# A hand-written order of mixing steps: decays ahead of the second pair's projections, modulation rounds among the projections, softmax steps right behind them

## The chip, the cores and the metric

The kernel runs on one core of one Trainium2 chip. The metric is the device time of one execution in microseconds (us); a lower number is better. The engines named below are PE (TensorE, matrix products and transposes), DVE (VectorE), ACT (ScalarE), POOL (GpSimd) and SP (SyncE, which here only issues DMAs). Each of them works through its own queue in order, so an instruction that waits holds up all that stands behind it on the same engine. ACT, POOL and SP can also issue DMAs, and such an issue stands in the same queue.

## What is computed

Two layers of a diffusion backbone, on 512 latent tokens and, in the first layer, 256 context tokens with the same weights. Width 1024. One layer, cut to what matters here:

```python
def modulation(cvec, w_mod, b_mod):
    m = (jax.nn.silu(cvec) @ w_mod + b_mod)[..., None, :]
    return jnp.split(m, 6, axis=-1)

def trunk_layer(x, cx, c, c_ctx, ...):
    sh1, sc1, ga1, sh2, sc2, ga2 = modulation(c, w_mod, b_mod)
    sh1c, sc1c, ga1c, sh2c, sc2c, ga2c = modulation(c_ctx[None], w_mod, b_mod)
    u = (rmsnorm(x, g_mix) * (1 + sc1) + sh1) @ w_in
    uc = (rmsnorm(cx, g_mix) * (1 + sc1c) + sh1c) @ w_in
    p, gq, gk, gv, gg, rf, rb, aq, ak, av = split_in(u)
    ...
    # gated linear attention, both directions: decay = exp(cumsum(log_sigmoid(r @ w_gate + b_gate) / 16))
    o_gl, _, _ = gla_bidir(*gla_features(gq, gk, gv, rf, rb, w_gate, b_gate), s_f, s_b)
    # softmax attention of 8 heads over 256 context + 512 latent keys
    mix = jnp.concatenate([pool_mixer(p, w_pool, s_pool),
                           gla_output(o_gl, gg, g_gla, x.dtype),
                           latent_attention(ql, k_all, v_all)], axis=-1) @ w_out
    x = x + ga1 * mix
    x = x + ga2 * squared_relu_mlp(rmsnorm(x, g_mlp) * (1 + sc2) + sh2, w_up, w_down)
    # the first layer does the same for the context: cx = cx + ga1c * mix_c, ...
```

## The kernel before

All weights are float32 and are multiplied in three passes: each weight tile is loaded by a DMA of SP into a buffer of the tag `raw` (3 buffers), ACT rounds it to a high part `whi` (line 159), DVE makes the low part `wlo` as the difference (line 78), and PE does high times high, high times low and low times high. `whi` and `wlo` live in rings of the tags `hi` and `lo`.

A layer has a mixing part (input projections, gated linear attention, softmax attention, pooling, output projection) and an MLP part. In the profile below the mixing parts lie at about 60 to 457 us and 1030 to 1335 us, the MLPs behind them. In the mixing part four generators are interleaved by a string of letters in the table `STEPS`, one string for each layer; each letter lets its generator go on to its next `yield`, and the code that it passes is issued at that place:

- `a`: the projections, one token tile of 128 at a time: gates, keys and values (`k_proj`), queries (`q_proj`), and the pooled part (`p_proj`); outputs of the token-wise ones are named `tm` (line 335), those of the others `fm` (lines 316 and 318).
- `g`: the gated linear attention, in two pairs of heads. For each pair: `decay` (2 steps: the decays from `rT`, tiles `z` and `tree`), `levels` (8 steps, for the widths 0, 1, 2, 4, ... 64: matmuls `att`, line 763, then four in-place products on DVE that grow the query and key tiles `QQ` and `KK`, line 720, and a masked copy to `dg`, line 783, or copies to `AT`), `states` (2) and `outputs` (2). The order is decay, levels and states of pair 0, decay of pair 1, outputs of pair 0, then levels, states and outputs of pair 1. A level's matmuls read what the level before has grown.
- `m`: in the first layer only, the two remaining modulation rounds. A round is 8 steps; each step loads 1 MB of `w_mod` as two tiles `rawm` (SP, line 188, into the rings `hi` and `lo` that the weights use) and multiplies them into the PSUM tile `pm` (line 190), 4 instructions of PE for each tile. At the end of a round `mod_end` loads the bias into the tile `brow`, adds `pm` (line 199), transposes it (line 202), writes `modT` and stores the gates to DRAM (`gaD`, line 209). The first layer's MLP holds three more rounds, those of the second layer (`modulation_sums`), which end in the same function.
- `t`: the softmax attention. The first step makes the key stack: transposes `kT`, then `kh` on ACT and `kl` on DVE (line 78); the second makes the first query stack: transposes `qT`, then `qs` on ACT and DVE (line 78). Scores `sc` are at line 1020, the row maxima `nmx` at 1023, the exponentials `p` at 1024, their transposes `pT` at 1038, and the products with the values `av` at 1047.

At each `t` the loop first finishes all that is left of `a` (`run(at_)`) and of `m` (`run(mods)`). A scheduler then sets the final order on each engine, in which an instruction can move past others that it doesn't depend on; the rows of each engine shown under the change are that final order.

The query and key projections of pair 1 (`qk_proj(1, 0)` and `qk_proj(1, 1)`) stand ahead of the interleaved part, in the first layer ahead of `rT`, the transposed gate inputs that the decays read, in the second layer right behind it.

Of the kernel before, what the change touches and what calls it, by code (L numbers as in the profile page):

```python
# [10 lines left out]
F32 = mybir.dt.float32  # L11
# [13 lines left out]
LEVELS = (1, 2, 4, 8, 16, 32, 64)  # L25
C_GV, C_GG, C_R, C_AQ = 768, 1024, 1280, 1312
GT = 5
STEPS = ("aggaamgmagagaaagaaaamgaaaaamagaaaagaaaaaagmgaaaagamggmggmgtt"
         "mggtttmtttgttgtmgtggtttgtttgttmgtmtgttmgtt",
         "ggggagaggaaagaaggaaaaaagaaaagaaaggaagaaggatatgatttttgaatgttg"  # L30
         "tttgggtttgttggttttgtttgt")


@with_exitstack
def hybrid_kernel(ctx, tc, x, c, cx, c_ctx, w_mod, b_mod, g_mix, w_in, w_pool, s_pool, w_gate, b_gate,
                  g_gla, g_q, g_k, w_out, g_mlp, w_up, w_down, g_final, k_mask, k_rope, k_edge, k_invw, out):
    nc = tc.nc
# [3 lines left out]
    lay = ctx.enter_context(tc.tile_pool(name="lay", bufs=1))  # L41
    wp = ctx.enter_context(tc.tile_pool(name="wp", bufs=5))
# [9 lines left out]
    def nm(s):  # L52
        uid[0] += 1
        return f"{s}_{uid[0]}"
# [137 lines left out]
        mod_end(l, r, modT, pm)  # L192

    def mod_end(l, r, modT, pm):
        brow = lay.tile([128, 512], F32, tag="brow", name=nm("brow"))
        for j in range(4):
            c0 = r * 2048 + j * 512
            nc.scalar.dma_start(brow[32 * j:32 * j + 32], b_mod[l, c0:c0 + 512].partition_broadcast(32))
        V.tensor_tensor(brow, pm, brow, ALU.add)
        pt = psC("pt")  # L200
        for cc in range(4):
            T.transpose(pt[:, cc * 128:(cc + 1) * 128], brow[:, cc * 128:(cc + 1) * 128], ident)
        V.tensor_copy(modT[:, r], pt.rearrange("p (c j r) -> p j c r", c=4, j=4)[:, :, :, 0:2])
        if r >= 1:
            which = r - 1
            for s in range(2):
                for jj in range(2):
                    row = 32 * (jj + (2 if r == 2 else 0)) + s
                    nc.scalar.dma_start(gaD[l, which, s:s + 1, jj * 512:(jj + 1) * 512], brow[row:row + 1, :])

    def modulation_sums(l, r, modT, streams):

# [174 lines left out]
    def run(g):  # L387
        for _ in g:
            pass
# [24 lines left out]
    for l in range(2):  # L414
# [169 lines left out]
        def qk_proj(pr, qk, ps=None):  # L584
            isk = qk == 1
            if ps is None:
                ps = psA("fm")
                fm_matmul(ps, wcols(W, 256 + qk * 256 + pr * 128, 128, 1), hT, KT, True, both or isk)
            if isk:
                KK[pr] = wide("KK")  # L590
                A.activation(KK[pr][:, 0:NT], ps[:, 0:NT], AF.Copy)
                G.tensor_copy(KK[pr][:, NT:2 * NT], KK[pr][:, 0:NT])
            else:
                gq[pr] = slot("gq")
                A.activation(gq[pr][:, 0:N_], ps[:, 0:N_], AF.Copy, scale=0.125)
# [14 lines left out]
        for t in alltiles:  # L610
# [3 lines left out]
                ps = psB("tm")  # L614
                tm_matmul(ps[:, 0:288], t, wk, hT, KT)
            A.activation(GU[:, t], ps[:, 0:288], AF.Copy)
        if l == 0:
            qk_proj(1, 0)
            qk_proj(1, 1)

        rT = gp.tile([32, NT], F32, tag="gt", name=nm("rT"), bufs=GT)
        ps = psA("rT")
        for t in alltiles:
            T.transpose(ps[0:32, t * 128:(t + 1) * 128], GU[:, t, 256:288], ident)
        A.activation(rT, ps[0:32, 0:NT], AF.Copy)
        if l == 1:
            qk_proj(1, 0)
            qk_proj(1, 1)

        if l == 0:  # L630
            load_params(1)
# [4 lines left out]
        def gate_proj(pr):  # L636

            wk = wcols(W, C_GG + pr * 128, 128, 1)
            ps = psA("fm")
            fm_matmul(ps, wk, hT, KT, True, both)  # L640
            g_ = slot("gate")
            gx, tmp = g_[:, 0:N_], gslot("sg", "gt", bufs=GT)[:, 0:N_]
            A.activation(gx, ps[:, 0:N_], AF.Copy)
            gate[pr] = g_
            yield
            V.tensor_scalar(tmp, gx, -87.0, None, ALU.max)
            A.activation(tmp, tmp, AF.Exp, scale=-1.0)
            A.activation(tmp, tmp, AF.Ln, bias=one)
            A.activation(tmp, tmp, AF.Exp, scale=-1.0)
            V.scalar_tensor_tensor(gx, tmp, gglaT, gx, ALU.mult, ALU.mult)  # L650
# [224 lines left out]
        def k_proj():  # L875
            wk = wcols(W, C_AQ + 512, 256, 2)
            UK = slot("UK")
            UKt.append(UK)
            UV = slot("UV")
            UVt.append(UV)  # L880
            for t in alltiles:
                ps = psB("tm")
                tm_matmul(ps[:, 0:256], t, wk, hT, KT)
                A.activation(UK[:, t * 128:(t + 1) * 128], ps[:, 0:128], AF.Copy)
                A.activation(UV[:, t * 128:(t + 1) * 128], ps[:, 128:256], AF.Copy)  # L885
                yield
            sq = gslot("sq", "gt", bufs=GT)
            head_norm(UK.rearrange("p (m e) -> p m e", e=64), sq.rearrange("p (m e) -> p m e", e=64), 12)
            yield
            rope_mult(UK[:, 0:NL].rearrange("p (t h e) -> p t h e", h=2, e=64), rk,  # L890
                      sq[:, 0:NL].rearrange("p (t h e) -> p t h e", h=2, e=64), 4, 2)
            kc = UK[:, NL:NT].rearrange("p (m e) -> p m e", e=64)
            V.tensor_tensor(kc, kc, gr[:, 1].unsqueeze(1).to_broadcast([128, 4, 64]), ALU.mult)
            yield

        def q_proj(cb):
            wk = wcols(W, C_AQ + cb * 256, 256, 2)
            for t in live:
                g = t // 3
                if t % 3 == 0:  # L900
                    Uq[cb][g] = slot("Uq")
                uq = Uq[cb][g]
                ps = psB("tm")
                tm_matmul(ps[:, 0:256], t, wk, hT, KT)
                A.activation(uq[:, (t % 3) * 256:(t % 3) * 256 + 256], ps[:, 0:256], AF.Copy)
                yield
                if t % 3 == 2 or t == live[-1]:
                    nt = t % 3 + 1
                    sq = gslot("sq", "gt", bufs=GT)[:, 0:nt * 256]
                    uv_ = uq[:, 0:nt * 256]  # L910
                    head_norm(uv_.rearrange("p (m e) -> p m e", e=64), sq.rearrange("p (m e) -> p m e", e=64), nt * 4, 0.125)
                    yield
                    nr = nt if g == 0 else 1
                    u4 = uv_.rearrange("p (t h e) -> p t h e", h=4, e=64)
                    s4 = sq.rearrange("p (t h e) -> p t h e", h=4, e=64)
                    rope_mult(u4[:, 0:nr], rq[:, :, 3 * g:3 * g + nr], s4[:, 0:nr], nr, 4)
                    if nr < nt:
                        qc = uq[:, nr * 256:nt * 256].rearrange("p (m e) -> p m e", e=64)
                        V.tensor_tensor(qc, qc, gr[:, 0].unsqueeze(1).to_broadcast([128, (nt - nr) * 4, 64]), ALU.mult)
                    yield  # L920
# [8 lines left out]
            yield  # L929

        def a_thread():
            for th in (gate_proj(0), gate_proj(1), k_proj(), q_proj(0), q_proj(1), p_proj(0), p_proj(1)):
                yield from th

# [175 lines left out]
        for ch in STEPS[l]:  # L1110
            if ch == "t":
                run(at_)
                run(mods)
            next(ths[ch], None)
        run(at_)
        run(mods)
# [77 lines left out]
        mods = iter(())  # L1194
# [127 lines left out]
```

## Time and profile before

| | |
|---|---|
| median of 3 runs | 1698.22 us (1693.12, 1698.79, 1698.22) |
| the profiled execution: its own time | 1700.61 us |
| the profiled execution: its span on the core | 1698.8 us |
| instructions | 28409 |
| PE busy | 1618.9 us (95%) |
| DVE busy | 911.1 us (54%) |
| ACT busy | 639.1 us (38%) |
| POOL busy | 408.3 us (24%) |
| mean DMA rate | 96 GB/s |
| first layer, mixing to the output projection | about 60 to 385 us |
| second layer, mixing to the output projection | about 1030 to 1279 us |

The busy shares are means over the whole span, and the stages have different limits: in the MLPs PE hardly ever waits, in the mixing parts it does. PE's clock is granted by a throttle and is shown as a share of full speed. A row of the waits names an engine and a line, what ended its wait, and then the microseconds in total, the times and the longest one.

### The profile page before, as it was taken

The page shows a single profiled execution, that of the slowest core. Times are in us where ns is not written, and L with a number is a line of the kernel's source. Part 1 is how long each engine was busy: PE and PEld are TensorE (multiplying, and loading weights), DVE is VectorE, ACT ScalarE, POOL GpSimd, SP SyncE. Part 2 cuts the span into 40 slices and gives each one's busy share as a digit, 9 for nine tenths or more (in the row PEclk, how much of TensorE's full clock was granted, in tenths as well). Part 3 has the DMA queues.
Part 4 walks back from the last instruction along what each step waited for, and adds up shares of the span by engine and source line. Part 5 has one row for each costly group of instructions (what it writes and reads, how often), then busy time and mean ns, then how long its engine had stood idle before and what let it go on. Part 6 is the DMA issues. An engine that isn't in the chain of part 4 may idle for free.

```text
span 1698.8 us, 28409 instructions
## 1 busy us (share of the span) xinstructions
PE 1618.9 (95%) x11899; PEld 1334.4 (79%) x11899; DVE 911.1 (54%) x1302; ACT 639.1 (38%) x1092; POOL 408.3 (24%) x468
## 2 busy tenths in 40 slices
PE   7999968899999999999999999997899999999997
PEld 4989636669978888888888888885669888888885
DVE  4437367753583546546555564486753545545454
ACT  5444246662442312213122234454662522222222
POOL 1111031202201231220311362242111212222225
PEclk9999989999999999999999999997999999999999
DMA  9422530204331313325334232100024223333321
GB/s 320 125 87 65 204 107 3 101 13 127 98 122 53 124 54 121 130 63 186 119 98 161 87 104 81 55 2 1 2 98 126 86 76 99 99 100 99 100 99 50
DMA packets 140255, 163.36 MB, mean 96 GB/s; under 512 B 9412, under 2 KB 116304, under 8 KB 140128
## 3 DMA queue, kind: packets, MB, share of 16 engines
q1 hardware_dynamic: 133312, 147.10, 27.2%
q10 hardware_dynamic: 6816, 14.46, 2.4%
q8 instruction: 93, 1.52, 0.4%
q14 instruction: 34, 0.28, 0.1%
HBM read 157.31 MB, written 4.23 MB: 95 GB/s over the span
## 4 chain that ended last, share of the span: by engine, by line
PE 88%; DVE 4%; ACT 3%; DMA 2%; issue 2%; POOL 1%; SPq 0%; POOLq 0%; DVEq 0%; ACTq 0%
PE dn L335 25%; PE up L316 19%; PE tm L335 8%; PE op L335 7%; PE up L318 5%; PE fm L316 4%; PE av L1047 3%; PE pT L1038 3%; PE up L325 2%; PE fm L318 2%; PE sc L1020 1%; DMA rawm<-in_w_mod_dram 1%; PE att L763 1%; PE pm L190 1%; PE sc L1021 1%
## 5 line engine op out<-in xcount | busy, mean ns | idle before, releaser
L159 ACT ACTIVATE whi<-raw 128x1024 fp32r<-128x1024 f32 (+2 forms) x182 | 184.9, 1031 | 581.2 <-PE dn L335 294.5
L1177 POOL TENSOR_TENSOR X<-X,rtmp 128x512 f32<-128x512 f32 x158 | 215.8, 1368 | 653.5 <-DVE rtmp L1176 653.1
L78 DVE TENSOR_TENSOR wlo<-raw,whi 128x1024 fp32r<-128x1024 f32 (+2 forms) x182 | 224.9, 1245 | 240.2 <-ACT whi L159 237.2
L1176 DVE TENSOR_TENSOR rtmp<-dn,ga 128x512 f32<-128x512 f32 x160 | 109.5, 688 | 215.9 <-PE dn L335 213.0
L335 PE MATMUL dn<-whi,al 128*128 128x512 f32 x480 | 187.2, 390 | 0.0
L335 PE MATMUL dn<-whi,ah 128*128 128x512 f32 x480 | 187.1, 390 | 0.0
L335 PE MATMUL dn<-wlo,ah 128*128 128x512 f32 x480 | 186.3, 390 | 0.0
L316 PE MATMUL up<-h2h,whi 128*128 128x512 f32 x464 | 182.6, 394 | 1.5 <-ACT relu L1219 1.5
L316 PE MATMUL up<-h2h,wlo 128*128 128x512 f32 x464 | 183.2, 395 | 0.0
L316 PE MATMUL up<-h2l,whi 128*128 128x512 f32 x464 | 182.8, 394 | 0.0
L335 PEld LDWEIGHTS dn<-whi,ah 128*128 128x128 f32 x480 | 90.2, 188 | 20.3 <-DVE rtmp L1176 0.8
L316 PEld LDWEIGHTS up<-h2h,whi 128*128 128x128 f32 x464 | 87.1, 188 | 23.5 <-ACT relu L1219 2.5
L335 PEld LDWEIGHTS dn<-whi,al 128*128 128x128 f32 x480 | 90.1, 188 | 19.5
L335 PEld LDWEIGHTS dn<-wlo,ah 128*128 128x128 f32 x480 | 90.1, 188 | 18.9
L316 PEld LDWEIGHTS up<-h2l,whi 128*128 128x128 f32 x464 | 87.1, 188 | 21.8 <-issue 2.5
L335 PE MATMUL tm<-whi,hTh 128*128 128x256 f32 (+1 forms) x352 | 102.3, 291 | 1.1 <-ACT UV L885 1.1
L316 PEld LDWEIGHTS up<-h2h,wlo 128*128 128x128 f32 x464 | 87.2, 188 | 19.6
L335 PE MATMUL tm<-whi,hTl 128*128 128x256 f32 (+1 forms) x352 | 100.8, 287 | 0.0
L335 PE MATMUL dn<-whi,a 128*128 128x512 f32 x320 | 100.0, 395 | 0.4 <-DVE rtmp L1176 0.4
L335 PE MATMUL tm<-wlo,hTh 128*128 128x256 f32 (+1 forms) x352 | 100.0, 287 | 0.0
L335 PE MATMUL op<-whi,mixh 128*128 128x256 f32 x320 | 91.2, 285 | 0.9 <-ACT whi L159 0.9
L335 PE MATMUL op<-wlo,mixh 128*128 128x256 f32 x320 | 90.2, 283 | 0.3 <-DVE wlo L78 0.3
(289 smaller groups left out, 3480.5 us busy)
## 6 DMA issues: line engine op xcount, KB each, us to landing
rawm<-in_w_mod_dram SPq DMA_DIRECT2D x80, 512.0 KB
raw<-in_w_up_dram SPq DMA_DIRECT2D x64, 512.0 KB
raw<-in_w_down_dram SPq DMA_DIRECT2D x64, 512.0 KB
raw<-in_w_in_dram SPq DMA_DIRECT2D x26, 512.0 KB
rawm<-in_w_mod_dram SPq DMA_DIRECT2D x32, 256.0 KB
raw<-in_w_out_dram SPq DMA_DIRECT2D x16, 512.0 KB
raw<-in_w_in_dram SPq DMA_DIRECT2D x12, 256.0 KB
ga<-gaD ACTq DMA_DIRECT2D x6, 512.0 KB
```

The source lines that it names most:

```text
L78: V.tensor_tensor(lo, full, hi.bitcast(F32), ALU.subtract)
L159: A.activation(hi, raw, AF.Copy)
L190: T.matmul(pm[32 * j:32 * j + 32, :], sstat[:, k, :], raw[:, (j % 2) * 512:(j % 2) * 512 + 512], start=(k == 0), stop=(k == KT - 1), skip_ ...
L316: T.matmul(ps[:, 0:NL], a, b[:, 0:NL], start=st, stop=sp_)
L318: T.matmul(ps[:, NL:NT], a, b[:, NL:NT], start=st, stop=sp_)
L325: T.matmul(ps[:, cs], a, b[:, cs], start=(k == 0 and i == 0), stop=(k == nk - 1 and i == 2))
L335: T.matmul(ps, a[:, sl], bb, start=(k == 0 and i == 0), stop=(k == nk - 1 and i == 2))
L763: T.matmul(ps[g * bw:(g + 1) * bw, o0:o0 + bw], a_, b_, start=True, stop=True)
L1038: T.transpose(pt_[:, i * 128:(i + 1) * 128], p_[:, ki * 128:(ki + 1) * 128], ident)
L1047: T.matmul(av_[64 * hh:64 * hh + 64, 0:256], vst, pe[:, hh * 256:hh * 256 + 256], start=(ki == 0), stop=(ki == len(kts) - 1))
L1176: V.tensor_tensor(tmp, ps, ga[0 if t < 4 else 1][:, sl], ALU.mult)
L1177: (V if b == NB - 1 and not both and t == 3 else G).tensor_tensor(X[t][:, sl], X[t][:, sl], tmp, ALU.add)
```

## The change

1. `STEPS` has two new strings. In the first layer the old string has 33 `a`, 17 `g` and 8 of its 14 `m` ahead of the first `t`; the new one has 35 `a`, 20 `g` and all of its 17 `m`. In the second layer the old string has 25 `a` and 17 `g` ahead of the first `t`, the new one 31 `a` and 22 `g`.
2. The query and key projections of pair 1 move to the head of the projection generator, so that `rT` and the decays of pair 0 come ahead of them.
3. `run(mods)` at each `t` goes; what is left of the rounds would be done behind the loop, where nothing is left.
4. `brow` in `mod_end` takes a buffer of the weights' ring `raw` in place of its own; its four loads of the bias go from ACT's queue to SP's, and the four stores of the gates (in rounds 1 and 2) from ACT's queue to POOL's.

```diff
-STEPS = ("aggaamgmagagaaagaaaamgaaaaamagaaaagaaaaaagmgaaaagamggmggmgtt"
-         "mggtttmtttgttgtmgtggtttgtttgttmgtmtgttmgtt",
...
+STEPS = ("agamagamgaamgaagmaagmagamagamagamagagamagamagagamagamgaamgaagmaagmagamagam"
+         "ttgtgttgtgttgtttgttgttttgttttgtt",
...
     def mod_end(l, r, modT, pm):
-        brow = lay.tile([128, 512], F32, tag="brow", name=nm("brow"))
+        brow = wp.tile([128, 1024], F32, tag="raw", name=nm("brow"), bufs=3)[:, 0:512]
         for j in range(4):
             c0 = r * 2048 + j * 512
-            nc.scalar.dma_start(brow[32 * j:32 * j + 32], b_mod[l, c0:c0 + 512].partition_broadcast(32))
+            nc.sync.dma_start(brow[32 * j:32 * j + 32], b_mod[l, c0:c0 + 512].partition_broadcast(32))
...
-                    nc.scalar.dma_start(gaD[l, which, s:s + 1, jj * 512:(jj + 1) * 512], brow[row:row + 1, :])
+                    nc.gpsimd.dma_start(gaD[l, which, s:s + 1, jj * 512:(jj + 1) * 512], brow[row:row + 1, :])
...
-        if l == 0:
-            qk_proj(1, 0)
-            qk_proj(1, 1)

         rT = gp.tile([32, NT], F32, tag="gt", name=nm("rT"), bufs=GT)
...
-        if l == 1:
-            qk_proj(1, 0)
-            qk_proj(1, 1)
...
         def a_thread():
+            for qk in range(2):
+                qk_proj(1, qk)
+                yield
             for th in (gate_proj(0), gate_proj(1), k_proj(), q_proj(0), q_proj(1), p_proj(0), p_proj(1)):
                 yield from th
...
             if ch == "t":
                 run(at_)
-                run(mods)
             next(ths[ch], None)
```

On SP in the first layer, these rows stood around the last weights of the projections (`raw`; two `rawm` make one modulation step):

```order
L188 DMA rawm_1758<-in_w_mod_dram 128x1024
L152 DMA raw_2301<-in_w_in_dram 128x8x128
L188 DMA rawm_2182<-in_w_mod_dram 128x1024
L188 DMA rawm_2186<-in_w_mod_dram 128x1024
L188 DMA rawm_2384<-in_w_mod_dram 128x1024
L188 DMA rawm_2388<-in_w_mod_dram 128x1024
L188 DMA rawm_2437<-in_w_mod_dram 128x1024
L188 DMA rawm_2441<-in_w_mod_dram 128x1024
```

Six `rawm` of the 32 stood ahead of the last projection weights, `raw_2301`, and 26 behind them; 20 of those follow on the rows shown, in one run. In the changed kernel the rows around the last weights of the projections are:

```order
L152 DMA raw_2619<-in_w_in_dram 128x8x128
L152 DMA raw_2684<-in_w_in_dram 128x8x128
L188 DMA rawm_2181<-in_w_mod_dram 128x1024
L188 DMA rawm_2185<-in_w_mod_dram 128x1024
L188 DMA rawm_2260<-in_w_mod_dram 128x1024
L188 DMA rawm_2264<-in_w_mod_dram 128x1024
L188 DMA rawm_2307<-in_w_mod_dram 128x1024
L188 DMA rawm_2311<-in_w_mod_dram 128x1024
L188 DMA rawm_2449<-in_w_mod_dram 128x1024
L198 DMA brow_2806<-in_b_mod_dram 32x512 x4
L188 DMA rawm_2453<-in_w_mod_dram 128x1024
```

Now 18 `rawm` stand ahead of the last two projection weights, spread among the weights before them, and 14 behind; the bias loads come from this queue too.

On PE, just ahead of the first scores `sc` of the first layer, stood before (`rg` belongs to the outputs of pair 0, `att_2753` to the second level of pair 1):

```order
L202 MATMUL pt_2648<-ident,brow_2642 128x128 x3
L827 MATMUL rg_2527<-ident,rsg_2518 64x128 x8
L827 MATMUL rg_2538<-ident,rsg_2518 64x128 x4
L202 MATMUL pt_2648<-ident,brow_2642 128x128
L1073 MATMUL qT_2683<-ident,Uq_1537 128x128 x3
L1073 MATMUL qT_2683<-ident,Uq_1701 128x128
L1073 MATMUL qT_2684<-ident,Uq_1701 128x128 x2
L1073 MATMUL qT_2845<-ident,Uq_1537 128x128 x3
L1073 MATMUL qT_2845<-ident,Uq_1701 128x128
L763 MATMUL att_2753<-QQ_2550,KK_965 32x32 x48
L1020 MATMUL sc_2814<-kh_2669,qs_2691 128x512
```

And in the changed kernel:

```order
L190 MATMUL pm_2034<-rawm_2798,sstat 32x512 x2
L190 MATMUL pm_2034<-rawm_2802,sstat 32x512 x2
L976 MATMUL kT_2826<-ident,UK_1177 128x128 x6
L1070 MATMUL qT_2847<-ident,Uq_1626 128x128 x3
L1070 MATMUL qT_2847<-ident,Uq_1924 128x128
L1070 MATMUL qT_2848<-ident,Uq_1924 128x128 x2
L1070 MATMUL qT_3142<-ident,Uq_1626 128x128 x3
L1070 MATMUL qT_3142<-ident,Uq_1924 128x128
L757 MATMUL att_2865<-QQ_2446,kc_2866 32x32 x12
L202 MATMUL pt_2812<-ident,brow_2806 128x128 x4
L757 MATMUL att_2865<-QQ_2446,kc_2866 32x32 x36
L1017 MATMUL sc_2928<-kh_2833,qs_2855 128x512
```

Between the last projection and the scores stood 21 tiles of the modulation and the first two levels of pair 1 before (the rows shown are the end of it); now two tiles of the modulation do, and the levels are the third and fourth of pair 1 (from the third on they read `kc`, a copy of the keys). The outputs of pair 0 are done ahead of it.

On DVE, up to the first `qs` that those scores read, stood before:

```order
L720 TENSOR_TENSOR KK_965<-KK_965,z_2421 128x384
L720 TENSOR_TENSOR QQ_2550<-QQ_2550,z_2448 128x384
L783 COPY_PREDICATED dg_2552<-mask_735,att_2753 128x192 x2
L720 TENSOR_TENSOR KK_965<-KK_965,tree_2429 128x192x2
L720 TENSOR_TENSOR KK_965<-KK_965,tree_2456 128x192x2
L78 TENSOR_TENSOR kl_2670<-kT_2662,kh_2669 64x768
L720 TENSOR_TENSOR KK_965<-KK_965,tree_2429 128x96x4
L720 TENSOR_TENSOR KK_965<-KK_965,tree_2456 128x96x4
L78 TENSOR_TENSOR kl_2676<-kT_2662,kh_2675 64x768
L720 TENSOR_TENSOR KK_965<-KK_965,tree_2429 128x48x8
L720 TENSOR_TENSOR KK_965<-KK_965,tree_2456 128x48x8
L78 TENSOR_TENSOR qs_2691<-qT_2683,qs_2691 64x512
```

And in the changed kernel:

```order
L714 TENSOR_TENSOR QQ_2446<-QQ_2446,tree_2226 128x192x2
L714 TENSOR_TENSOR QQ_2446<-QQ_2446,tree_2279 128x192x2
L777 COPY_PREDICATED dg_2448<-mask_735,att_2741 128x192 x2
L199 TENSOR_TENSOR brow_2806<-pm_2034,brow_2806 128x512
L78 TENSOR_TENSOR kl_2834<-kT_2826,kh_2833 64x768
L203 COPY modT_124<-pt_2812 128x32
L383 SCALAR_TENSOR_TENSOR scT_125<-modT_124,vec 128x8 x2
L714 TENSOR_TENSOR QQ_2446<-QQ_2446,tree_2226 128x96x4
L714 TENSOR_TENSOR QQ_2446<-QQ_2446,tree_2279 128x96x4
L777 COPY_PREDICATED dg_2448<-mask_735,att_2865 128x192 x2
L78 TENSOR_TENSOR kl_2840<-kT_2826,kh_2839 64x768
L78 TENSOR_TENSOR qs_2855<-qT_2847,qs_2855 64x512
```

The products that grow `KK` here for the widths 1 to 8, and the two for the width 16 right behind these rows, stand further ahead now, beside the last projections; the products of `QQ` for the widths 2 and 4 stand here in their place, and the bias add `brow` has come in between.

More of the change, by code (lines that the diff above doesn't have):

```diff
@@ L27 @@
 GT = 5
-STEPS = ("aggaamgmagagaaagaaaamgaaaaamagaaaagaaaaaagmgaaaagamggmggmgtt"
-         "mggtttmtttgttgtmgtggtttgtttgttmgtmtgttmgtt",
-         "ggggagaggaaagaaggaaaaaagaaaagaaaggaagaaggatatgatttttgaatgttg"
-         "tttgggtttgttggttttgtttgt")
+STEPS = ("agamagamgaamgaagmaagmagamagamagamagagamagamagamagamgaamgaagmaagmagamagam"
+         "ttgtgttgtgttgtttgttgttttgttttgtt",
+         "agagaagagaagagaagagagaagagaagagaagagagaagagaagagaagag"
+         "ttgttgttgtttgtttgttttgttt")
 @with_exitstack
```

## The prediction

> **What bounds the kernel now.** I read the page first, then the windows by stage, then the waits of PE and of SP's queue, then the timelines around the two longest waits. On the page stand the span, PE's busy share in 40 slices and the chain that ended last:
>
> ```profile
> span 1698.8 us, 28409 instructions
> PE   7999968899999999999999999997899999999997
> PE 88%; DVE 4%; ACT 3%; DMA 2%; issue 2%; POOL 1%; SPq 0%; POOLq 0%; DVEq 0%; ACTq 0%
> ```
>
> PE makes 88% of the chain. A change that adds and removes no matmul can only take from the other 12%. Where they lie is seen in the windows (PE busy with its count, PEld, DVE, ACT, POOL, granted clock, DMA share, GB/s):
>
> ```profile
> 60.00:175.00 115.00, 115.00 (x1440) 103.33 (x1438) 54.31 (x91) 50.93 (x92) 17.86 (x34) 1.00 0.30 90
> 175.00:232.00 57.00, 53.00 (x493) 31.24 (x491) 21.20 (x48) 15.24 (x28) 8.29 (x18) 0.94 0.63 215
> 232.00:385.00 153.00, 128.56 (x1543) 90.68 (x1541) 102.17 (x176) 96.22 (x218) 30.02 (x48) 0.92 0.11 39
> 457.00:1000.00 543.00, 539.05 (x2771) 452.09 (x2770) 297.28 (x320) 138.08 (x164) 132.09 (x106) 1.00 0.34 112
> 1150.00:1280.00 130.00, 113.33 (x1243) 78.82 (x1242) 82.37 (x147) 79.50 (x164) 19.51 (x32) 0.92 0.12 42
> ```
>
> In the projections (60 to 175) PE is never idle. In 175 to 232 it is idle for 4.0 us, in the first layer's softmax stage for 24.4, in the second layer's for 16.7, each at a clock below 1. The first layer's MLP idles 4.0 us in 543. So 45 us at most are to be had in the stages that the change reorders, beside what the clock costs. What PE waits for, first layer (60 to 385), then second layer (1030 to 1290):
>
> ```profile
> PE sc L1020 <- DVE qs L78: 11.2, 1, 11.2
> PE sc L1020 <- ACT p L1024: 5.1, 4, 1.9
> PE pm L190 <- DMA rawm<-in_w_mod_dram: 3.9, 3, 3.5
> ...
> PE sc L1020 <- DVE qs L78: 4.5, 1, 4.5
> PE kT L979 <- ACT pm L927: 2.9, 1, 2.9
> PE att L763 <- ACT p L1024: 2.6, 3, 1.0
> ```
>
> Two single waits stand out in the first layer, 11.2 and 3.5 us; in the second the start of the softmax takes 4.5 and 2.9.
>
> **The 3.5 us wait, and what goes with it.** PE's timeline there, and from the chain a block of the same matmuls that waits for nothing:
>
> ```profile
> 174.11 1.06 PE L190 MATMUL pm<-rawm,sstat 128*32 128x512 f32 x8
> 181.19 1.92 PE L190 MATMUL pm<-rawm,sstat 128*32 128x512 f32 x4 [3.47 <-DMA rawm<-in_w_mod_dram]
> 184.26 0.63 PE L316 MATMUL fm<-hTl,whi 128*128 128x512 f32 x1
> 186.18 0.63 PE L316 MATMUL fm<-hTl,whi 128*128 128x512 f32 x1
> 187.47 0.40 PE L316 MATMUL fm<-hTl,whi 128*128 128x512 f32 x1
> 203.56 2.70 PE pm L190 x20
> ```
>
> The twenty matmuls of 174.11 to 183.11 (181.19 and its 1.92) take 9.0 us and cost 2.70 where nothing waits: 6.3 lost. Up to about 186.7 the projection's matmuls show 0.63 for what takes 0.40 later, and start every 0.43 instead of 0.23 us: half clock for 3.25 us, 1.6 lost. Together **7.9 us**. The cause is on SP's queue (60 to 240), whose waits are grouped by what freed the buffer:
>
> ```profile
> SPq L188 <- PE tm L335: 36.7, 4, 20.3
> SPq L188 <- PE pm L190: 23.2, 9, 16.0
> ```
>
> The modulation tiles use the weights' own buffers; one stood 20.3 us until a projection had read its weights. Once free, many loads come at once: DMA share 0.63 in 175 to 232 against 0.30 before. The new order puts 18 of the 32 tiles ahead of the last weights instead of 6. That moves 12 x 0.52 = 6.3 MB into a stretch that moved 90 GB/s x 115 us = 10.4 MB; 16.7 MB in 115 us are 145 GB/s, about half of the DMA engines' time by the share of that row (0.30 x 16.7 / 10.4 = 0.48). So the tiles can come in time, the burst behind the projections is gone, and I take all of the 7.9 off. Ends: nothing, if one tile is still late by as much, to 7.9.
>
> **The 11.2 us wait.** DVE in that stretch, then the prices of what stands there after the change, the last PE rows and the clock by windows of 10 us:
>
> ```profile
> 235.73 1.69 DVE L720 TENSOR_TENSOR QQ<-QQ,z 128x384 f32<-128x384 f32 x1 [0.68 <-PE att L763]
> 238.28 0.62 DVE L783 COPY_PREDICATED dg<-mask,att 128x192 f32<-128x192 int32 x2
> 238.97 1.94 DVE L720 TENSOR_TENSOR KK<-KK,tree 128x384 f32<-128x384 f32 x2
> 241.82 1.65 DVE L720 TENSOR_TENSOR KK<-KK,tree 128x384 f32<-128x384 f32 x2
> 243.51 0.96 DVE L78 TENSOR_TENSOR kl<-kT,kh 64x768 fp32r<-64x768 f32 x1
> 244.39 1.65 DVE L720 TENSOR_TENSOR KK<-KK,tree 128x384 f32<-128x384 f32 x2
> 246.07 1.02 DVE L78 TENSOR_TENSOR qs<-qT,qs 64x512 fp32r<-64x512 f32 x2
> L720 DVE TENSOR_TENSOR QQ<-QQ,tree 128x384 f32<-128x384 f32 x12 | 6.5, 571 | 5.7 <-PE att L763 5.7
> 233.45 1.25 PE L1073 MATMUL qT<-ident,Uq 128*128 128x128 f32 x10
> 234.63 1.06 PE L763 MATMUL att<-QQ,KK 64*32 64x32 f32 x96
> 1158.80 0.92 PE L979 MATMUL kT<-ident,UK 128*128 128x128 f32 x6 [2.89 <-ACT pm L927]
> 240.00:250.00 10.00, 3.10 (x10) 2.57 (x10) 9.77 (x15) 7.63 (x12) 2.99 (x6) 0.50 0.01 2
> 250.00:260.00 10.00, 5.74 (x117) 4.56 (x116) 9.65 (x17) 4.83 (x11) 0.72 (x4) 0.75 0.00 1
> ```
>
> Ahead of `qs` DVE grows `KK` for four widths in a row; that `KK` is not what the scores read, it only stands ahead of them in the queue. After the change these products lie beside the last projections. Behind the last projection PE then has a level (1.06), two modulation tiles (8 matmuls at 2.70 / 20, 1.1), `kT` (0.92), `qT` (1.25), four transposes of the bias tile (0.75, about 0.6 of `qT`'s row) and a level (1.06): 6.1 us. When that level is done, DVE still has two products of `QQ` (2 x 0.57), `dg` (0.62), `kl` (0.96) and `qs` (1.02): 3.7 us, which is PE's new idle time; everything before these on DVE fits into the 6.1. The saving is 11.2 - 3.7 = **7.5 us**. Ends: `kl` and `qs` alone (2.0, saving 9.2) and twice the estimate (7.4, saving 3.8), should DVE come into this stretch late.
>
> The clock is a separate matter. After 3.5 us of idle time it was half (181 to 186.7), and after the 11.2 us it was 0.50 and 0.75 in the two windows shown. With 3.7 us I expect it to halve again, so nothing is taken off for it.
>
> A rule of the Trainium skill bears on this point. TensorE: Matmul & The Clock Gate, in its part on the HAM clock gate, puts the fall to half clock after about 3.4 us of idle time and the return after about 3.4 us of sustained work. The trace agrees on the fall (3.47 us sufficed), while its return took 5.5 us. By that page an idle time of a little less than the 3.7 estimated here would keep full clock, and by the 5.5 us at half rate the sum would then be 2.7 us lower.
>
> **The rest of the first softmax stage.** In 250 to 260 PE is busy for 5.74 us and DVE for 9.65: DVE still sets the pace, with the backlog of `KK` and `QQ`. Without the eight products of `KK` (12 of them stood in this stage, below: 732 ns each, so 5.9 us) DVE reaches the row maxima earlier. Of the 4.3 us idle there I take **3 us** off; ends 0 and 5.9.
>
> ```profile
> L720 DVE TENSOR_TENSOR KK<-KK,tree 128x384 f32<-128x384 f32 x12 | 8.5, 732 | 0.1
> PE att L763 <- DVE QQ L720: 0.5, 1, 0.5
> 231.20 1.16 ACTq L209 DMA_DIRECT2D gaD<-brow  x4
> ```
>
> **What the projections pay.** Three more levels and the bias add now stand among them. DVE had 54.3 of 115 and 21.2 of 57 us to do there, so there is room; but each level reads what the one before has grown, and PE waits in order. A level is a chain of 1.06 (PE), 4 products at 0.57 and `dg` 0.62, some 4 us; twenty steps of this thread in about 150 us leave 7.5 us each, against 10 before (17 in 172). Where the spacing falls short, the nearest row is the wait of 0.5 us above. Four of them, **+2 us**; ends 0 and 8 (one stall like the 7.9).
>
> **Second layer.** No modulation runs there. The start now has `kT` and the scores behind levels four to six of pair 1; priced the same way, `kh` and `kl` twice, eight copies to `AT` on ACT and `qs` make about 7 us of idle time, as the 4.5 + 2.9 = 7.4 of before, so nothing is gained at the start. Behind it three level steps are left instead of eight. Of the 16.7 us idle in that stage 7.4 belong to the start; of the other 9.3, I take **4 us** off (5 of 8 levels gone, at 9.3 x 5 / 8 = 5.8, less a third for waits that stay between `sc`, `nmx` and `p`). Ends 0 and 9.
>
> **What I cost at nothing.** The moved `qk_proj` change only places. On ACT the stores of the gates took 1.16 us for four and delayed it ahead of `ogl`, but PE was still busy with the modulation; POOL, which takes them, is busy for 30 of 153 us. No row shows such an issue on POOL: between none and four times ACT's 1.16, beside that slack. `brow` in the weights' ring leaves two of three buffers to the weights for a few us, once in each of five rounds; in the MLP the DMA share is 0.34 and PE idles 4.0 of 543 us, so 0. The upper end is a late weight in each of the MLP's three rounds at 3.5 us, 10 us.
>
> **Sum.** -7.9 - 7.5 - 3 + 2 - 4 = -20.4 us. The profiled execution took 1700.6 us, the median of three 1698.2; the same change from the median gives **1678 us**, 1.2% less. What a measurement can tell from no change is about 0.5%, 8.5 us.
>
> **Rivals.**
>
> 1. *Only the late tiles are cured.* The scores come earlier, but DVE is then just as late: it has nearly the same work (102 of 153 us) in a shorter time, and the 11.2 us come back in pieces. For it: DVE at 9.7 of 10 us around the start. Against: the products that stand ahead of `qs` are really fewer. 1698.2 - 7.9 = 1690 us.
> 2. *Slower: the modulation tiles hold up SP's queue ahead of weights.* A tile may only be loaded when a projection has given up its buffer, and the weights of a later projection now stand behind it in SP's queue in 12 more cases. The row with 20.3 us shows that such a wait is long. If weights then come late, PE stands still in the middle of the projections, where it never waited before, and each such stall has the measured price of 7.9 us, half clock and all. It turns the sum from the third one on and is past 0.5% with four: 1678 + 31.6 = 1710 us. Against it: the order asks for every weight before the tiles that follow it, and 115 us of projections without a wait show that weights come early.
> 3. *Nothing comes of it.* The time won at the two waits is given back at the end of the stage, because with fewer levels to fill in, PE waits for ACT and DVE (`p` and `nmx`) between scores: 5.1 us of such waits stand there now, and they would have to grow fourfold. 1697 us.
>
> **How the numbers follow.** Forecast 0.60, rival 1 0.17, rival 2 0.10, rival 3 0.13. Faster by over 0.5% is below 1689.7: the forecast and half of rival 1, 0.69. Slower: rival 2, 0.10. Within 0.5%: the rest, 0.21. The range takes the larger ends of the terms on the good side (7.9 + 9.2 + 5.9 + 9 without a cost would be 1666; a little below it if the clock holds, 1663) and on the bad side rivals 1 and 3 with a margin, 1702; it leaves rival 2 out.
>
> **What would show it.** The wait of `pm` for `rawm` is gone, and no wait over 1 us stands in the projections (steps one and four). The first `sc` of the first layer waits for 2 to 5 us, with `QQ` and not `KK` ahead of `qs` on DVE. The stage from that `sc` to the output projection is shorter by some 3 us, and that of the second layer by some 4. The MLPs keep their length to 1 us. A `tm` or `fm` that waits for `wlo` or a load, or MLPs that are longer, would make the prediction wrong.

## The result, and the profile after

| | median | runs | lowest to highest |
|---|---|---|---|
| before | 1698.31 us | 4 | 1693.12 to 1698.79 |
| changed | 1707.12 us | 4 | 1706.6 to 1707.72 |

The ratio is 1.0059, 95% interval 1.0039 to 1.0079: the changed kernel is 0.6% slower, where 1.2% faster was forecast. The profiled execution took 1707.13 us, 6.5 more than that of before. The span on the page and PE's busy time, which has hardly changed (1618.9 before):

```profile
span 1704.9 us, 28427 instructions
PE 1620.6 (95%) x11899; PEld 1336.7 (78%) x11899; DVE 911.3 (53%) x1302; ACT 639.6 (38%) x1092; POOL 415.7 (24%) x484
```

The windows of the changed kernel, with the columns of those shown of before:

```profile
60.00:175.00 115.00, 113.15 (x1464) 93.75 (x1463) 56.57 (x102) 49.61 (x92) 18.92 (x32) 1.00 0.48 161
175.00:232.00 57.00, 56.48 (x782) 43.16 (x780) 30.96 (x60) 23.95 (x38) 17.25 (x29) 1.00 0.24 76
232.00:385.00 153.00, 135.23 (x1310) 96.67 (x1311) 95.03 (x159) 93.33 (x213) 27.49 (x48) 0.94 0.16 54
457.00:1000.00 543.00, 539.05 (x2731) 450.29 (x2730) 293.46 (x315) 139.56 (x168) 139.96 (x118) 1.00 0.34 110
1030.00:1150.00 120.00, 107.36 (x1297) 94.38 (x1296) 65.89 (x124) 54.06 (x105) 28.72 (x56) 0.93 0.13 36
```

The first layer looks as it was meant to. In 175 to 232 PE is idle for 0.5 us instead of 4.0, at full clock, and the DMA share of the projections rose from 0.30 to the forecast 0.48. The last row stands for the second layer's projections: PE idled 2.3 us of these 120 before (117.73 busy, row below), now 12.6, and the clock fell to 0.93. PE's waits, first layer (60 to 385), then second layer (1020 to 1180):

```profile
PE sc L1017 <- ACT p L1021: 5.5, 4, 1.8
PE sc L1017 <- DVE qs L78: 4.1, 1, 4.1
PE pT L1035 <- ACT p L1021: 2.6, 1, 2.6
PE pm L190 <- DMA rawm<-in_w_mod_dram: 1.3, 1, 1.3
...
PE sc L1017 <- DVE qs L78: 6.1, 1, 6.1
PE kbt L688 <- DVE KK L714: 4.5, 1, 4.5
PE tm L335 <- ACT UV L879: 2.6, 1, 2.6
PE att L757 <- ACT kc L738: 2.1, 1, 2.1
PE att L757 <- DVE QQ L714: 1.9, 3, 0.9
PE att L757 <- DVE KK L714: 1.7, 2, 1.3
```

The two single waits of the first layer shrank (`qs` 11.2 to 4.1, `rawm` 3.9 to 1.3); the waits of the scores for `p` did not (5.1 before, 5.5 now). In the second, a series of waits for the level chain has come, ahead of a softmax start that waits about as long as before.

Where the span went is seen best from four marks in each trace: the first `op` of the first layer, the first `tm` of the second layer, its first `op`, and the end. All later comparisons use the same marks:

| us | to the first layer's `op` | to the second layer's `tm` | to its `op` | to the end |
|---|---|---|---|---|
| before | 384.3 | 648.0 | 246.8 | 419.7 |
| changed | 372.9 | 647.3 | 265.7 | 419.0 |
| difference | -11.4 | -0.7 | +18.9 | -0.7 |

The first layer's mixing won 11.4 us, the MLPs stayed, and the second layer's mixing lost 18.9. Between the first `rT` and the first `sc` of the second layer the trace before has 111.9 us, the changed one 136.0; from there to `op` the changed one has 108.8 against 114.1. The stretch from `rT` to `sc` in the windows, changed and before:

```profile
1041.10:1177.10 136.00, 113.70 (x1530) 97.32 (x1528) 78.50 (x159) 62.02 (x125) 31.52 (x56) 0.92 0.11 32
```

```profile
1053.10:1165.00 111.90, 102.43 (x1210) 87.68 (x1207) 66.91 (x131) 56.72 (x112) 33.36 (x53) 0.98 0.14 39
```

PE idles 22.3 us there instead of 9.5, 12.8 more. It works at half clock for 15.4 us instead of 1.0; half of the difference, an estimate of 7.2 us, is lost by that. The 320 more matmuls are five more levels of pair 1, 3.8 us at 0.76 each. Together that is 23.8 of the 24.1 us.

The worst place is at 1104 to 1118 us. PE's timeline there in the changed kernel, then DVE's and ACT's (start, duration, engine, line, what, and in brackets the idle time ahead of it with what ended it):

```profile
1104.69 0.76 PE L757 MATMUL att<-QQ,kc 64*32 64x32 f32 x64
...
1108.69 0.33 PE L757 MATMUL att<-QQ,KK 64*64 64x64 f32 x4 [1.35 <-DVE KK L714]
1109.40 0.68 PE L757 MATMUL att<-QQ,KK 64*64 64x64 f32 x28 [0.38 <-DVE KK L714]
1114.63 3.12 PE L688 MATMUL kbt<-ident,KK 128*128 128x128 f32 x12 [4.55 <-DVE KK L714]
```

```profile
1108.80 0.55 DVE L714 TENSOR_TENSOR KK<-KK,tree 128x384 f32<-128x384 f32 x1
...
1111.51 0.17 DVE L260 SCALAR_TENSOR_TENSOR rsa<-rsa,ssa 128x12 f32<-128x12 f32 x1 [1.70 <-ACT rsa L258]
...
1112.33 0.96 DVE L867 TENSOR_TENSOR Uq<-Uq,rsa 128x768 f32<-128x768 f32 x1
...
1113.54 0.95 DVE L714 TENSOR_TENSOR KK<-KK,tree 128x384 f32<-128x384 f32 x1
```

```profile
1109.29 0.30 ACT L257 ACTIVATE rsa<-ssa,epsc 128x12 f32<-128x12 f32 x1
1109.50 1.73 ACT L770 ACTIVATE AT<-att 32x128 f32<-32x128 f32 x8
1111.26 0.21 ACT L258 ACTIVATE rsa<-rsa 128x12 f32<-128x12 f32 x1
```

The last three levels of pair 0 and the transposes `kbt` follow each other on PE with no projection tile in between. The first of the three doesn't wait; the other two and `kbt` each wait for a product on DVE, 7.2 us together (0.93, 1.73 and 4.55). The last product stands on DVE behind the query norm (`rsa`, `Uq`), which waits 1.70 us for ACT, where eight copies to `AT` stand between the norm's two steps. In the trace before, 3.1 to 4.0 us of projections stood between any two of these levels and ahead of `kbt`, and none of them waited:

```profile
1107.33 0.76 PE L763 MATMUL att<-QQ,kc 64*32 64x32 f32 x64
...
1111.44 0.76 PE L763 MATMUL att<-QQ,KK 64*32 64x32 f32 x64
...
1116.02 0.69 PE L763 MATMUL att<-QQ,KK 64*64 64x64 f32 x32
...
1119.63 1.47 PE L694 MATMUL kbt<-ident,KK 128*128 128x128 f32 x12
```

PE's clock pays as well. The same 10 us in the windows of the changed kernel, then of before, here with the row of the whole stretch:

```profile
1110.00:1120.00 10.00, 5.36 (x41) 4.49 (x38) 7.19 (x15) 3.53 (x12) 3.08 (x4) 0.50 0.01 2
```

```profile
1110.00:1120.00 10.00, 10.00 (x168) 9.62 (x167) 8.63 (x17) 8.11 (x26) 2.54 (x4) 1.00 0.01 3
...
1030.00:1150.00 120.00, 117.73 (x1269) 104.24 (x1270) 67.43 (x132) 58.97 (x118) 36.21 (x64) 1.00 0.14 40
```

### The profile page after: what moved, and what is told of

It is laid out like the page before. It is cut to its first block, busy times and chain, and to the rows that moved or that the text cites. A ratio compares the mean times of both kernels' runs of the same rounds, so it can differ in the third digit from the quotient of the medians.

```text
span 1704.9 us, 28427 instructions
## 1 busy us (share of the span) xinstructions
PE 1620.6 (95%) x11899; PEld 1336.7 (78%) x11899; DVE 911.3 (53%) x1302; ACT 639.6 (38%) x1092; POOL 415.7 (24%) x484
```

## The experiments

Each run is compared with runs of the kernel before on the same chip; the medians of before beside them were 1697.98, 1700.01 and 1697.08 us, so ratios are the surer numbers. Medians and ratios, and the marks of each profiled execution:

| run | median us | ratio, 95% interval | first layer's `op` | second layer's `tm` to `op` |
|---|---|---|---|---|
| before | | 1 | 384.3 | 246.8 |
| changed | 1707.12 | 1.0059 (1.0039 to 1.0079) | 372.9 | 265.7 |
| e1_l2_old | 1687.65 | 0.9927 (0.9913 to 0.9941) | 374.0 | 244.7 |
| e2_l2_new_alone | 1713.69 | 1.0085 (1.0070 to 1.0100) | 381.4 | 263.8 |
| e5_l2_spaced | 1699.50 | 0.9997 (0.9987 to 1.0008) | 372.9 | 257.5 |
| e7_l1_mod_alone | 1699.20 | 1.0005 (0.9992 to 1.0017) | 382.6 | 244.8 |
| e6_l1_levels_burst | 1694.47 | 0.9971 (0.9960 to 0.9983) | 378.2 | 246.3 |
| e4_brow_back | 1704.85 | 1.0033 (1.0021 to 1.0046) | 372.4 | 262.8 |
| e10_l2_early_levels | 1687.31 | 0.9931 (0.9919 to 0.9943) | 373.8 | 244.1 |
| e11_stacks_early | 1687.03 | 0.9938 (0.9926 to 0.9951) | 374.4 | 244.1 |
| e12_brow_back | 1686.41 | 0.9938 (0.9925 to 0.9950) | 370.2 | 246.1 |
| e13_l2_gates_first | 1701.61 | 1.0023 (1.0014 to 1.0033) | 372.2 | 261.2 |

A mark comes from one execution. Where PE's rows are the same it still moves by 2 to 3 us (first layer: 384.3 before, 381.4 in e2; second layer: 244.1 in e10, 246.1 in e12), so smaller differences between marks say little.

**The second layer as before, and its change alone.** First the changed kernel with the second layer's part undone:

```diff
-         "agagaagagaagagaagagagaagagaagagaagagagaagagaagagaagag"
-         "ttgttgttgtttgtttgttttgttt")
+         "ggggagaggaaagaaggaaaaaagaaaagaaaggaagaaggatatgatttttgaatgttg"
+         "tttgggtttgttggttttgtttgt")
...
         A.activation(rT, ps[0:32, 0:NT], AF.Copy)
+        if l == 1:
+            qk_proj(1, 0)
+            qk_proj(1, 1)
...
-            for qk in range(2):
+            for qk in range(2 if l == 0 else 0):
```

> The changed kernel with the second layer as before (its old string in STEPS, its two qk_proj behind rT again); the first layer's new order, the bias tile in the weights' ring and the moved DMAs stay. Theory (the second layer's order costs what is lost): the second layer gives back the 18.7 us by which it became longer, so 1707.1 - 18.7 = about 1688 us, 10 us under before. Rival 1 (the ring, the queues or the earlier end of the first layer spoil the second layer whatever its order): still 1700 us or more. Rival 2 (half of it is the order): about 1697 us.

And the reverse, the kernel before with this part alone:

> The kernel before with nothing but the second layer's part of the change (new second string, its two qk_proj at the head of the projections). Theory: the first layer is as before and the second one longer by 18.7 us: about 1717 us, more than the whole change costs. Rival 1 (the loss needs the bias tile in the ring or the first layer's new order): 1698 us.

1687.65 and 1713.69 us: both on the side of the theory. The second layer's order alone costs 0.85% (14 us; 17.0 by the marks), less than the 18.7 expected, and the rest of the change alone gains 0.73% (12 us). The loss needs neither the ring nor the first layer.

**Which part of the second layer's order.** In the first try its letters are shifted, with a projection tile that has matmuls behind each late level of pair 0:

```diff
-         "agagaagagaagagaagagagaagagaagagaagagagaagagaagagaagag"
-         "ttgttgttgtttgtttgttttgttt")
+         "agagaagagaagagaagaaagagagaaagaaagagagaaagaagaggaga"
+         "ttgttgttgttgttgttgttgttgttttt")
```

> The changed kernel with the letters of the second layer's new string shifted, so that each level of pair 0 from the fourth on has a projection tile with matmuls behind it; ahead of the first t stand 31 a and 19 g instead of 31 a and 22 g. Theory (PE stands still because levels follow each other with no projection in between): the 7.0 us of waits at the last levels of pair 0 and the half clock behind them (3 to 5 us) go, about 1695 to 1698 us. Rival (too much work for DVE and ACT among these projections, however it is spread): within 3 us of 1707.

1699.5, 0.6% less than the changed kernel by the two ratios and 1.5 us above the theory's range: the rival falls, but 10.7 us of the second layer's loss stay (257.5 against 246.8). The levels start as late here as in the change, 36.7 us behind `rT` (23.7 before), so the late start alone doesn't make the loss: from `rT` to `sc` 11.7 us came back (136.0 to 124.3), 2.3 of them for three levels of pair 1 that now stand behind that `sc`. The cover is still short: in PE's order 14 matmuls stand between the last two levels, and none between the last one and `kbt`. Waits that are left, second layer:

```profile
PE sc L1015 <- DVE qs L76: 7.1, 1, 7.1
PE tm L333 <- ACT UV L877: 2.6, 1, 2.6
PE kbt L686 <- DVE KK L712: 2.0, 1, 2.0
```

Two suspects are left: the early part of the string, and the levels of pair 1 ahead of the softmax. The second layer of e1 was given three such levels among its last projections, the rest as before:

```diff
-...gaagga" "tatgatttttgaatgttgtttgggtttgttggttttgtttgt"
+...gaagga" "aagagaga" "ttttttttttgtttgggtttgttggttttgtttgt"
```

> The kernel with the first layer's new order and the second layer's old one (1687.7), but with three levels of pair 1 of the second layer put among its last projections instead of behind the first softmax steps; the levels of pair 0 and the gates keep their old places. Theory (the loss that is left in the spaced order, 12 us, comes from the early part: gates in one piece ahead of the levels, and ACT late for the keys): 1685 to 1690. Rival (levels of pair 1 ahead of the softmax cost what they were to save, since they put DVE work ahead of qs): 1693 or more.

1687.31 us, a ratio of 0.9931 beside e1's 0.9927: the levels of pair 1 cost nothing there and bring nothing. The first `sc` behind them waits longer (6.8 us instead of 4.6), behind it 4.3 us come back (112.0 to 107.7 from there to `op`). Nearly as many steps stand ahead of the softmax here as in the change (20 `g` against 22). So the loss is in where the steps of pair 0 stand. The sharpest form of that is one edit in e10: the two gate projections ahead of the first seven `g` and not among them, as the change has them:

```diff
-"ggggagaggaaagaaggaaaaaag...
+"aagggggggaaagaaggaaaaaag...
```

> The fastest version so far (1687.3) with one edit in the second layer's string: its two letters for the gate projections (11.5 us of matmuls) stand ahead of the first seven letters g instead of among them, as they do in the change. Number and kind of steps ahead of the softmax are the same. Theory (a projection covers a level's wait only if its letter stands behind that level): the levels start later, the last three stand in a row again, and 4 to 9 us are lost, 1691 to 1696. Rival (only the number of levels ahead of the softmax counts): 1687 within 2.

1701.61 us, 14 us more than e10 (0.9% by the ratios), past the upper end of the theory's range: the direction and the place are the theory's, the size is more than twice its middle. From `rT` to `sc` PE idles 19.6 us instead of 11.9, at a mean clock of 0.89 instead of 0.98. PE's waits ahead of the softmax in e10 (1020 to 1150), then in e13 (1020 to 1160):

```profile
PE att L758 <- DVE dg L778: 1.7, 1, 1.7
PE tm L333 <- ACT UV L880: 1.0, 1, 1.0
```

```profile
PE tm L333 <- ACT UV L880: 3.6, 1, 3.6
PE kbt L689 <- DVE KK L715: 3.5, 1, 3.5
PE att L758 <- DVE KK L715: 1.8, 2, 1.4
```

Right behind these stretches both wait for `qs` (6.8 and 7.6 us), and e13 has e10's wait for `dg` (1.7) there too. The row of `kbt` with its wait for the last growth of `KK` is back, and the one of `tm` for `UV` has grown. PE's order says why. In e10 each gate projection lies between two levels (level 0, 24 matmuls, level 1, 24 matmuls, level 2); in e13 and in the changed kernel the gates are used up ahead of level 0, the later levels use up the tiles of the first queries, and the last levels run out of cover: in the changed kernel the last three stand in a row, in e13 the last two, with 15 matmuls ahead of them. The edit also lets level 0 begin later (35.0 us behind `rT` instead of 23.7); e13 alone can't tell that from the missing cover; e5, with the late start and more cover, speaks for the cover.

**The first layer's two parts.** The modulation alone, spread in the kernel before, with `a` and `g` left in their places:

```diff
-"aggaamgmagagaaagaaaamgaaaaamagaaaagaaaaaagmgaaaagamggmggmgtt" "mggtttmt...
+"amggamagamgagamaamgaamaamgaamaaamagamaamagamaamaamaggamaamagamggggg" "ttggttt...
```

> The kernel before with nothing changed but the place of the letters m in the first layer: all 17 are spread among the projections as in the new string, a and g stay where they were. By the prediction's first term the late tiles alone are worth 7.9 us: about 1690 us, with the 11 us wait of the first scores still there. Rival (the waits only move, since PE works through the same matmuls and meets the softmax just as late for DVE): 1696 to 1699 us. If spreading alone puts late weights into the projections: over 1700 us.

1699.2 us, no difference. PE's rows with a wait between 222 and 244 us in that run:

```profile
224.35 1.62 PE L814 MATMUL ss<-blk,o 128*128 128x2 f32 x12 [3.06 <-ACT o L808]
227.88 1.09 PE L761 MATMUL att<-gq,KK 64*32 64x32 f32 x82 [1.91 <-DVE ssg L816]
242.91 0.77 PE L1018 MATMUL sc<-kh,qs 128*128 128x512 f32 x1 [8.14 <-DVE qs L76]
```

The late tiles are gone (the waits for `rawm` are 0.2 us), but the burst of modulation had also been the work that covered the outputs of pair 0. Without it PE waits there for ACT (`o`) and DVE (`ssg`), 5.0 us in two pieces, and then still 8.1 us for `qs`. Besides, the late tiles cost less than one profile said: in e2, whose first layer has the order of before row for row, the same place shows

```profile
PE sc L1018 <- DVE qs L76: 11.2, 1, 11.2
PE pm L188 <- DMA rawm<-in_w_mod_dram: 2.5, 3, 1.6
```

and a granted clock of 1.00 in 175 to 232; its first layer reaches `op` 2.9 us earlier. Then the counterpart, the first layer's new order with the burst: every second of the first 16 `m` stays, nine stand right ahead of the first `t`; second layer as before.

```diff
-"agamagamgaamgaagmaagmagamagamagamagagamagamagamagamgaamgaagmaagmagamagam" "ttgt...
+"agaagamgaagaagmaagagamagaagamagagaagamagaagamgaagaagmaagagamaga" "mmmmmmmmm" "ttgt...
```

> The changed kernel with the second layer as before and with the modulation of the first layer not spread: 8 of its 17 letters stand among the projections, 9 right ahead of the first t, so that a burst comes behind the last projection again. Everything else of the first layer's new order stays. Spreading alone gave nothing (1699.2), the first layer's whole new order 10.3 us (1687.7). If the gain is that of the levels ahead of the softmax by itself: about 1688 to 1690. If the two need each other (the burst in front of the scores again, and the levels have to fill for what it filled): about 1696. The prediction's sum of terms, 7.5 without the 7.9: about 1691.

1694.47 us (0.9971), between the sum of terms and the case that the two need each other. By the ratios the levels alone gain 0.29%, the spreading alone nothing (1.0005), and both together 0.73% (e1), so the gains do not add up one by one. In the old order the burst covers the outputs of pair 0 (e7). In e6 the first `sc` waits for nothing and starts no later than in e1 (235.6 and 236.4 us), but late tiles are back (3.4 us of waits for `rawm`) and 20 of the 128 `pm` matmuls stand between the scores; from there to `op` it takes 142.6 us against 137.6. How much each of these costs was not separated.

**The bias tile and its queues.** In the changed kernel:

```diff
-        brow = wp.tile([128, 1024], F32, tag="raw", name=nm("brow"), bufs=3)[:, 0:512]
+        brow = lay.tile([128, 512], F32, tag="brow", name=nm("brow"))
...
-            nc.sync.dma_start(brow[32 * j:32 * j + 32], b_mod[l, c0:c0 + 512].partition_broadcast(32))
+            nc.scalar.dma_start(brow[32 * j:32 * j + 32], b_mod[l, c0:c0 + 512].partition_broadcast(32))
...
-                    nc.gpsimd.dma_start(gaD[l, which, s:s + 1, jj * 512:(jj + 1) * 512], brow[row:row + 1, :])
+                    nc.scalar.dma_start(gaD[l, which, s:s + 1, jj * 512:(jj + 1) * 512], brow[row:row + 1, :])
```

> The changed kernel with the bias tile in its own buffer and its loads and stores on ACT's queue again; the order is that of the change. The prediction cost these at nothing: 1707 us within 3. If the ring costs late weights in the MLP or in the projections: 1700 or less.

1704.85 us, inside the 3 us; by the ratios it is 0.26% less than the changed kernel (some 4.4 us), with intervals that overlap. The 2.9 us that the second layer is shorter there come with rows of PE that the scheduler put elsewhere. So the same edit was made in e10, where PE's rows of the second layer keep their places:

> The fastest version so far (1687.3) with the bias tile in its own buffer and its loads and stores on ACT's queue again. On PE the second layer's rows stand as in that version, unlike in the run with the whole change, where the order shifted by a few rows. The prediction's cost of nothing: within 2 us of 1687. Rival (the ring and POOL's stores cost the 2 to 3 us that the other run showed): 1684 to 1685.

1686.41 us; the ratio is 0.9938 beside 0.9931, with intervals that cover each other. The price is nothing that these runs can tell.

**A shorter start of the softmax.** A first form of this, e9, also put two `t` of the second layer ahead of its last three `a`; that order ends in a deadlock, so it has no time. In e10 the first layer's first two `t` were moved ahead of the letters of `p_proj` (and `run(at_)` left out, with all `a` in the string):

```diff
-"...gaagmaagmagamagam" "ttgtgttg...
+"...gaagmaagmag" "tt" "amagam" "gtgttg...
...
-            if ch == "t":
-                run(at_)
             next(ths[ch], None)
```

> The fastest version so far (the first layer's new order, the second layer with pair 0 as before and three levels of pair 1 among its last projections: 1687.3), and in the first layer the key stack and the first query stack ahead of the two last projections (p_proj) instead of behind them. If the wait of the first scores (4.1 us, with half clock behind it) is the chain kT, kh, kl, qs behind the last projection, those 11 us of matmuls cover it: 1681 to 1685 us. If DVE is late there anyway: 1686 to 1689.

1687.03 us: no gain, the second of the two. PE's waits between 215 and 260 us, in the changed kernel and then in this run:

```profile
PE sc L1017 <- DVE qs L78: 4.1, 1, 4.1
PE sc L1017 <- ACT p L1021: 2.9, 2, 1.8
PE pT L1035 <- ACT p L1021: 2.6, 1, 2.6
```

```profile
PE sc L1018 <- ACT p L1022: 3.6, 2, 2.9
PE att L758 <- DVE dg L778: 2.3, 1, 2.3
PE att L758 <- DVE QQ L715: 1.5, 1, 1.5
```

The wait for `qs` is gone, and the levels behind it wait for DVE by nearly as much (3.8 us). In this stretch DVE is busy for 9.54 of 10 us in the changed kernel and in e10, and for 8.12 in e11. The row of the changed kernel:

```profile
240.00:250.00 10.00, 7.17 (x190) 5.90 (x191) 9.54 (x18) 4.58 (x11) 1.19 (x4) 0.68 0.01 2
```

## Why the prediction was wrong

The direction was wrong, and the step that failed is the cost of the levels among the projections. It was worked out for the first layer only ("twenty steps of this thread in about 150 us leave 7.5 us each ... +2 us"), and for the second layer nothing was set down between the first `rT` and the start of the softmax. An average spacing was compared with the length of one level's chain. What counts is the cover of each single level: the change leaves the last three of pair 0 with none. From `rT` to `sc` the second layer became 24.1 us longer: 12.8 us of idle time, some 7.2 of half clock and 3.8 of five more levels. The last two levels of pair 0 and `kbt` wait for 7.2 of the 12.8; the others are waits of the same kind in pair 1 (`kc` 2.1, `QQ` 0.9, `dg` 0.6), those in the outputs of pair 0 (`ss` and `rg`, 2.7) and that of `tm` for `UV` on ACT (1.5 more than before).

In sum, of the forecast -20.4 us the first layer fell short by 5.0 and the second by 22.9; with the 1.4 that the MLPs took less, that is the +6.1 us between the two spans.

Point by point:

- **First layer, late tiles (-7.9).** Wrong as a term by itself. The DMA share is as forecast, and of the waits for `rawm` one of 1.3 us is left where none was expected; but spreading alone moved the time by nothing (e7): the burst that was late was also cover. The 7.9 us were read from one execution, and another with the same order shows 2.5 us of waits at full clock (e2).
- **First layer, start of the softmax (-7.5).** Right: 3.7 us of wait were forecast, 4.1 came (11.2 before), and the rows of `qs` say so. That the clock would fall again was right too (0.68 in 240 to 250).
- **First layer, rest of the stage (-3).** Wrong: from `sc` to `op` it takes 137.2 us, 137.4 before, with 13.7 us idle, 13.2 before. In 250 to 260 DVE did become freer (5.60 busy instead of 9.65), but PE's waits there are mostly for `p` on ACT, 8.5 us in both traces; taking products from DVE did not shorten them.
- **First layer, the levels among the projections (+2).** Smaller: PE idles 1.85 us in 60 to 175, 1.3 of it for `rawm`, and 0.5 behind, so the levels cost about 1.1. In sum the first layer gained 11.4 us where the terms gave 16.4.
- **Second layer (-4).** Behind the first `sc` it gained 5.3, near the forecast; at the start the wait is 6.1 for `qs`, about as forecast. By the `att` rows seven levels stood behind that `sc` and two do now, where the working has eight and three. The loss ahead of it was not in the sum.
- **What was cost at nothing.** Right: the MLPs' marks agree within 0.7 us, and e12 shows no price of ring and queues.

Of the rivals, the third ("given back") named the right kind of thing, work moved away from where it covered a wait, at the wrong place. The second had the right sign, stalls among projections with half clock behind, but in the first layer and for the wrong reason: no weight came late in the projections of either. The clock rule cited from the Trainium skill, TensorE: Matmul & The Clock Gate, did not decide anything: the wait of 4.1 us is past its 3.4 and the clock fell, as in the sum. As a limit the traces don't bear it out: in the trace before, the clock fell some 2 us into the wait of 3.47 (0.97 in 178 to 180, 0.50 in 180 to 182), and behind a wait of 2.63 us in the changed kernel it was half too (last section).

The change is two changes of opposite sign: the first layer's part gains about 0.7%, the second layer's loses about 0.85% by itself. Kept apart they give a kernel faster than both (e1, e10 and e12, 1686 to 1688 us, 0.6 to 0.7% under before).

What stays open: how much of the second layer's 24 us each single wait makes by itself, with the half clock behind it, beyond what e5, e10 and e13 separate; and whether DVE's load alone keeps the first softmax from starting faster in e11, which was only argued from its busy share.

## What to carry to other kernels

Moving work earlier in an order that several threads share is two moves: that work comes earlier, and the chain that it covered where it stood is left bare. For each step of a chain, name the work that lies between it and the next one, and compare that with the chain's own length on all its engines; a mean over the stretch doesn't show it. Price the same change in each stage that it touches, and prove the parts apart, since one profile can show the gain and the loss of two stages as no difference.

## What the runs showed of the hardware

Waits of PE cost more than themselves, since the clock falls. Around the wait of 4.55 us in the changed kernel it was 0.50 (1110 to 1120), and the twelve transposes behind it took 3.12 us where the same twelve took 1.47 before. But a single long wait isn't needed. This clock had fallen as that wait began: 0.98 in 1109 to 1110, 0.50 in 1110 to 1111, behind four waits of 0.17 to 1.35 us, 2.66 together. Behind waits of 1.21 and 1.51 us it was 0.52 (1144 to 1147), and behind one wait of 2.63 us, that of `tm` for `UV`, it was half:

```profile
1083.00:1086.00 3.00, 3.00 (x16) 3.00 (x15) 0.67 (x1) 0.00 (x0) 2.21 (x7) 0.50 0.00 0
```

In e2 three waits of 0.23 to 1.64 us, 2.47 together, left it at 1.00. So no length of one wait up to which the clock holds comes out of these traces.

An issue of a gate store costs POOL more time than ACT, without any effect that e12 could tell; minimum, median and maximum in ns, changed and before:

```profile
L209 POOL DMA_DIRECT2D gaD<-brow x16: 484/484/725, 161.9 to 947.2; - x16
```

```profile
L209 ACTq DMA_DIRECT2D gaD<-brow x16: 222/258/275, 207.2 to 956.6; - x16
```
